# Moving rows of fp32 products in two halves of a tile, even columns in one and odd columns in the other

## The chip, the cores and the metric

The kernel runs on one core of a Trainium2 chip, as one program. The metric is device time in microseconds (us), the median of several runs. The core has engines with queues of their own: TensorE (PE) for matrix products, VectorE (DVE) and ScalarE (ACT) for elementwise work, SyncE (SP) whose queue issues nearly all transfers, and GpSimd (POOL), which is unused here. PE reads its operands from the on-chip memory SBUF, which has 128 partitions, and adds up results in banks of PSUM.

## What is computed

One layer of a streaming encoder on 1024 tokens of 1024 features, all in float32.

```python
h = h + 0.5 * swiglu_ffn(rmsnorm(h, norm_ffn1), ffn1_w_in, ffn1_w_out)
u = rmsnorm(h, norm_mix)
proj = u @ w_in
q, k, v, g_ret, p, gates = jnp.split(proj, split_points, axis=-1)
ret = retention(rotary(q), rotary(k) * RET_QK_DIM ** -0.5, v)
ret = ret * lax.rsqrt(jnp.mean(ret * ret, axis=-1, keepdims=True) + NORM_EPS)
ret = ret.reshape(b, s, RET_V) * jax.nn.silu(g_ret)
pool_out = multiscale_pool(p, pool_w, pool_scale)
gate = jax.nn.sigmoid(gates.reshape(b, s, N_BRANCH, D_MODEL) + gate_bias)
merged = gate[:, :, 0] * (ret @ w_ret_up) + gate[:, :, 1] * (pool_out @ w_pool_up)
h = h + merged @ w_out
h = h + 0.5 * swiglu_ffn(rmsnorm(h, norm_ffn2), ffn2_w_in, ffn2_w_out)
return rmsnorm(h, norm_final)
```

The feed-forward layers have 2816 hidden features, the retention 4 heads of 256.

## The kernel before

Features lie along the partitions and tokens along the columns: an activation is 8 tiles of 128 features by 1024 tokens. A product on PE has a stationary operand of 128 x 128 (the weights) and a moving operand of 128 x 512 (activations, 512 tokens of 128 features); its result adds to a PSUM bank of 128 x 512.

Float32 products are made of three products each. `split` (L160) writes a high part in the type float32r with a copy on ACT (L161), and the rest, source minus high part, with a subtraction on DVE (L162). `split_scaled` (L164) does the same with a factor per partition (L165 on ACT, L166 on DVE). `mm3` (L179) then adds three products: high by high (L181), high weights by low columns (L182), low weights by high columns (L183). PE loads 128 x 128 weights anew for each (PEld in the profile).

A moving operand is a tile of `mv` (L108), `[P, 2, H]`: 512 columns of the high part, 2048 bytes, and behind them the 512 columns of the low part. `parts(m)` gives the two, each read from its first column to its last. Weights lie in a tile of `wt` (L111) of four blocks of 128 columns for each part. A weight tile can be shifted in its place by `APART` = 22 columns, 88 bytes; this is done for the weights of `common` and for the operands of the retention that `pieces` cuts.

The stages, in order: feed-forward 1 (`ffn_in`, `ffn_out`), the projections (`values` and `pairs` of groups `project`), the retention with the pooling products put between (`retention`, `fillers`), merging and output projection (`two_by_two`), feed-forward 2. Large products go by Strassen's scheme with seven products in place of eight (`strassen`, steps `b1` to `b7`): `Next` makes the sums of activation blocks that they need, as moving operands, with `put` and `blocks`, and `prep_w` makes the sums of weights. Some of the seven are cut once more into products of 256 columns (`common`), whose moving operands are halves of such rows. `ffn_out` makes its moving operands with `operand` from spilled tiles. In `values` the roles are turned: the weights of the value projection are the moving operand, and the activations of 128 tokens at a time are loaded as weights, so results have tokens along the partitions; `store` spills them to DRAM, and `Unit.loads` reads them for the retention. In the retention itself q, k and v are made into rows with `operand` and read as weights and as moving operands.

The order of the work is set by the order of the code: `Flow.run` calls the preparing half of a step four steps ahead of its products (`LOOK` = 4) and takes deferred work from a queue, one or two items after each step. A tile scheduler lays the instructions on the engines by that order, with `high_priority` for what empties PSUM banks. Tiles come from rotating buffers: 28 of `mv`, 5 of `wt`, 4 of `raw`, 9 of `t4`, 8 of `c2`, and 8 PSUM banks.

Of the kernel before, what the change touches and what calls it, by code (L numbers as in the profile page):

```python
# [17 lines left out]
P = 128  # L18
# [72 lines left out]
def block_kernel(ctx: ExitStack, tc, x, x_tok, vecs, f1_in, f1_out, w_in, w_v, pool_w, w_ret, w_pool, w_o,  # L91
# [16 lines left out]
    def mv(name):  # L108
        return sb.tile([P, 2, H], F32R, tag="mv", bufs=N_MV, name=name)

    def wt(name, at=0):  # L111

        w = sb.tile([P, S + LINE], F32R, tag="wt", bufs=N_WT, name=name)
        return w[:, at : at + S].rearrange("p (z i c) -> p z i c", z=2, i=4)
# [35 lines left out]
        return t[:, j * H : (j + 1) * H]  # L150

    LO, HI = slice(0, HD), slice(HD, H)

    def half_of(t, j):
        return t[:, (LO, HI)[j]]
# [10 lines left out]
        stt(lo, src, by, hi.bitcast(F32), MUL, SUB)  # L166

    def operand(src, name):
        m = mv(name)
        split(m[:, 0], m[:, 1], src)  # L170
        return m
# [100 lines left out]
    class Next(Norm):  # L272
# [13 lines left out]
            self.square(mt, tokens, src)  # L286

        def put(self, n, i, src, by=None):
            m = mv(f"{self.name}{n}{i}")
            self.M[n, i] = m  # L290
            if by is None:
                split(m[:, 0], m[:, 1], src)
            else:
                split_scaled(m[:, 0], m[:, 1], src, by)

        def g(self, mt, v=None):
            if self.gain is None:
# [63 lines left out]
        def blocks(self, R, tags, over=False):  # L361

            left, x = dict(zip(("y3", "y2", "y4") if over else ("y1", "y3", "y2", "y4"), tags)), {}

            def sums(z):
                for i in range(2):
                    m = self.M[R, 2 * i + z]  # L370
                    v = c2(f"{self.name}x{i}{z}")
                    tt(v, m[:, 0].bitcast(F32), m[:, 1].bitcast(F32), ADD)
                    x.update({(i, j, z): half_of(v, j) for j in range(2)})

            def difference(n, z):

                x00, x01, x10, x11 = (x[i, j, z] for i in range(2) for j in range(2))
                to, p, q = {"y1": (x00, x01, x00), "y3": (x01, x11, x01), "y2": (x00, x11, x00),
                            "y4": (x00, x10, x00)}[n]
                tt(to, p, q, SUB)  # L380
                if n not in left:
                    m, at = self.M[R, z], HI
                else:
                    tag, bufs = left[n]
                    if (R, n) not in self.made:

                        self.made[R, n] = sb.tile([P, 2, H], F32R, tag=tag, bufs=bufs, name=f"{self.name}{R}{n}")
                    m, at = self.made[R, n], (LO, HI)[z]
                self.Y[R, n, z] = parts(m, at)
                split(m[:, 0, at], m[:, 1, at], to)  # L390
                if z and n == "y4":
                    self.ready.add(R)

            work = []
            for z in range(2):
                work.append(lambda z=z: (sums(z), difference("y1", z)))
                work.append(lambda z=z: difference("y3", z))
                work.append(lambda z=z: (difference("y2", z), difference("y4", z)))
            return work

        def block(self, R, n, z):

            if isinstance(n, str):
                flow.until(lambda: R in self.ready)
                return self.Y[R, n, z]
            return parts(self.operand(R, 2 * n[0] + z), (LO, HI)[n[1]])

        def work(self, *steps):

# [31 lines left out]
    def strassen(nx, wa, wb, name, evac, end, begin=None, shared=(), dest=None):  # L441
# [34 lines left out]

        def prod(dst, w, m, start, stop):
            for i in range(4):
                mm3(t[dst], parts(t["w", w], i), parts(nx.operand(m, i)), start and i == 0, stop and i == 3)

        def u(n):
            t[n] = c2(f"{name}{n}")
# [207 lines left out]
    def plain(M, nk, src, name, evac, begin, banks):  # L690

        t = {}
        for q in range(0, nk, 4):

            def prep(q=q):
                if q == 0:
                    t["raw"] = raw(f"{name}raw")
                    load(t["raw"][:, : nk * P], src)
                t[q] = weights(t["raw"][:, q * P : (q + 4) * P], f"{name}w{q}")
                if q + 4 == nk:  # L700
                    begin()

            def body(q=q):
                if q == 0:
                    t["dst"] = [f(f"{name}d{j}") for j, f in enumerate(banks)]
                for i in range(4):
                    w = parts(t[q], i)
                    m = [parts(M(q + i)[j]) for j in range(2)]
                    first, final = q + i == 0, q + i == nk - 1
                    for j in range(2):  # L710
                        mm(t["dst"][j], w[0], m[j][0], start=first, stop=False)
                        mm(t["dst"][j], w[0], m[j][1], start=False, stop=False)
                    for j in range(2):
                        mm(t["dst"][j], w[1], m[j][0], start=False, stop=final)
                if q + 4 == nk:
                    evac(t["dst"])

            yield prep, body
# [85 lines left out]
    def plain_group(nx, blocks, name, evac, end):  # L804

        t, w = {}, {}

        def step(o, i, j):


            def prep():
                if j == 0:
                    w[o, i] = weights(blocks[2 * o + i], f"{name}w{o}{i}")

            def body():
                if i == 0:
                    t[o] = bank(f"{name}{o}{j}")
                for k in range(4):
                    mm3(t[o], parts(w[o, i], k), parts(nx.operand(("R11", "R12", "R21", "R22")[2 * i + j], k)),
                        i == 0 and k == 0, i == 1 and k == 3)  # L820
                if i == 1:
                    evac((o, j), t[o], None)
                    if (o, j) == (1, 1):
                        end()

            return prep, body

        return [step(o, i, j) for j in range(2) for i in range(2) for o in range(2)]
# [4 lines left out]
    def ffn_out(nx, ops, ready, w, res, name, sink, end, last=None):  # L833
# [100 lines left out]
        def step(n, f, k, where, start, after):  # L934
            o = {}

            def prep():
                L, X = f(k)
                o["w"] = weights(L, f"{name}{n}w{k}")
                o["m"] = X if len(X.shape) == 3 else operand(X, f"{name}{n}m{k}")  # L940
                if n == "p3" and not last and k >= FH // 2:
                    z = k - FH // 2 + 1
                    ahead[z] = operand(t4s(z), f"{name}p4m{z}")

            def body():
                if start and k == 0:
                    for i in range(4):
                        bk[where, i] = (sum_bank if where == "b" and i < N_SUM else bank)(f"{name}{n}{where}{i}")
                for i in range(4):
                    mm3(bk[where, i], parts(o["w"], i), parts(o["m"]), start and k == 0, k == FH - 1)  # L950
                    if k == FH - 1:
                        after(i)

            return prep, body
# [81 lines left out]
        L, X = {}, {}  # L1036

        def turned(n, k):
            mm3(last.bank(n), parts(X[k], slice(n * P, (n + 1) * P)), parts(L[k]), False, k == FH - 1)

        def near(k):
            def prep():
# [204 lines left out]
    def values():  # L1247
# [36 lines left out]
        def step(L, R, k, where, start, after):  # L1284
            w = []

            def prep():
                t = weights(block(L, k), f"v{L}w{k}")
                w.extend(flat(t, z) for z in range(2))

            def body():
                if start and k == 0:
# [1 line left out]
                        bk[where, i] = (sum_bank if where == "b" and i < N_SUM else bank)(f"v{L}{i}")  # L1294
                m = nx.operand(R, k)
                for i in range(4):
                    mm3(bk[where, i], parts(m, slice(i * P, (i + 1) * P)), w, start and k == 0, k == 3)
                    if k == 3:
                        with soon():
                            after(i, bk[where, i])  # L1300
# [1 line left out]
            return prep, body  # L1302

        def store(o, j, i, src):
            to = vs[2 * o + j].rearrange("p (h t c) -> p h t c", h=2, t=4)
            load(to[:, :, i], src.rearrange("p (h c) -> p h c", h=2))
            if i == 3:
                stored.update(f"v{h}{j}" for h in (2 * o, 2 * o + 1))

# [71 lines left out]
    def pool(n):  # L1381
# [13 lines left out]
        def body():  # L1395
            for i in range(2):
                mt = 2 * n + i
                dst = [f(f"px{mt}{j}") for j, f in enumerate((sum_bank, bank))]
                for kt in range(2):
                    for j in range(2):  # L1400
                        mm3(dst[j], parts(w[0], 2 * kt + i), parts(Mg[kt][j]), kt == 0, kt == 1)
                M[mt] = []
                for j in range(2):
                    m = mv(f"po{mt}{j}")
                    with soon():
                        split_scaled(m[:, 0], m[:, 1], dst[j], vec[:, V_SCALE + mt : V_SCALE + mt + 1])
                    M[mt].append(m)

        return prep, body
# [67 lines left out]
    class Unit:  # L1477
# [42 lines left out]
            self.dec, self.ss, self.O, self.state, self.total, self.by = u.dec, u.ss, u.O, u.state, u.total, u.by  # L1520

        def values(self):
            self.V = [operand(half(self.src["v"], n), f"v{self.name}{n}") for n in range(2)]
            if self.nh == 0:
                self.by = sb.tile([P, 32], F32, tag="by", bufs=2, name=f"by{self.h}")
                for j in range(2):
# [10 lines left out]
            return col(self.by, z + 4 * (j % 2) + 2 * self.nh + j // 2)  # L1537

        def operands(self):
            self.Q = [operand(half(self.src["q"], i), f"q{self.name}{i}") for i in range(2)]  # L1540
            self.K = [operand(half(self.src["k"], i), f"k{self.name}{i}") for i in range(2)]

        def scores(self):

# [470 lines left out]
```

## Time and profile before

| | |
|---|---|
| median of 3 runs | 2138.09 us (2138.02 to 2139.77) |
| span of the profiled execution, first to last instruction | 2137.8 us |
| PE busy, products | 2127.8 us, 10798 instructions |
| PE busy, loading weights | 1808.3 us |
| DVE busy | 1873.2 us, 3352 instructions |
| ACT busy | 1100.9 us, 2082 instructions |
| mean granted PE clock | 0.999 |
| memory traffic | 313.60 MB, 147 GB/s on average |

The profile is one execution, as the hardware profiler saw it. Durations of products overlap, since they are pipelined: PE takes the next one while the last drains, so the time that a product costs is the distance from its start to the next start, not its duration. An idle time of an engine costs only what the chain to the end waits for.

### The profile page before, as it was taken

To read this page: it belongs to the slowest core of one execution; us is meant where nothing else is said; L and a number is where in the kernel's file an instruction comes from. 1 tells how busy PE (TensorE), PEld (TensorE's weight loads), DVE (VectorE), ACT (ScalarE), POOL (GpSimd) and SP (SyncE) were. 2 spreads that over 40 slices of the span, in tenths; PEclk is the share of its full clock that TensorE was granted. 3 is DMA by queue.
4 is the path that set the end of the run, shared out by engine and by line. 5 is a ranking of instruction groups with operands and counts; after the bars stand their busy time and mean duration, and the time that the engine had idled before them with its cause. 6 is when DMAs were issued, how large, how long until landed. Compare 5 with 4: busy or idle time off the path is not lost.

```text
span 2137.8 us, 30138 instructions
## 1 busy us (share of the span) xinstructions
PE 2127.8 (100%) x10798; PEld 1808.3 (85%) x10798; DVE 1873.2 (88%) x3352; ACT 1100.9 (51%) x2082; POOL 0.2 (0%) x4
## 2 busy tenths in 40 slices
PE   9999999999999999999999999999999999999998
PEld 7888888888888888888888998888888888888887
DVE  8798888997986799999988988899988988899796
ACT  8544444454654534454457753456644544455454
POOL 0000000000000000000000000000000000000000
PEclk9999999999999999999999999999999999999999
DMA  7232323675543333332336666624133232358542
GB/s 251 83 133 75 138 84 129 202 266 187 172 138 98 110 109 119 109 124 104 119 129 223 197 226 236 236 89 163 64 103 119 87 126 85 132 199 276 192 138 99
DMA packets 116391, 313.60 MB, mean 147 GB/s; under 512 B 12817, under 2 KB 17041, under 8 KB 116241
## 3 DMA queue, kind: packets, MB, share of 16 engines
q1 hardware_dynamic: 115664, 310.63, 42.7%
q8 instruction: 84, 1.38, 0.3%
q10 hardware_dynamic: 576, 1.05, 0.1%
q14 instruction: 67, 0.54, 0.1%
HBM read 220.93 MB, written 90.70 MB: 146 GB/s over the span
## 4 chain that ended last, share of the span: by engine, by line
PE 94%; DVE 4%; ACT 1%; DMA 1%; issue 0%; SPq 0%; ACTq 0%; DVEq 0%
PE c_b L181 2%; PE c_b L182 2%; PE c_b L183 2%; PE a_b L181 2%; PE a_b L182 2%; PE a_b L183 2%; PE c_e L182 2%; PE c_e L181 2%; PE c_e L183 2%; PE a_e L182 2%; PE a_e L181 2%; PE a_e L183 2%; PE a_a L181 1%; PE a_a L183 1%; PE a_a L182 1%; PE c_a L181 1%
## 5 line engine op out<-in xcount | busy, mean ns | idle before, releaser
L182 PE MATMUL c_b<-n3T,c_wS 128*128 128x512 f32 x176 | 68.6, 390 | 0.0
L183 PE MATMUL c_b<-n3T,c_wS 128*128 128x512 f32 x176 | 68.5, 389 | 0.0
L181 PE MATMUL c_b<-n3T,c_wS 128*128 128x512 f32 x176 | 68.4, 390 | 0.0
L182 PE MATMUL a_b<-n1T,a_wS 128*128 128x512 f32 x168 | 65.4, 389 | 0.0
L181 PE MATMUL a_b<-n1T,a_wS 128*128 128x512 f32 x168 | 65.4, 389 | 0.0
L183 PE MATMUL a_b<-n1T,a_wS 128*128 128x512 f32 x168 | 65.3, 389 | 0.0
L181 PE MATMUL a_a<-n1R,a_wL 128*128 128x512 f32 x120 | 46.7, 389 | 0.0
L182 PE MATMUL a_a<-n1R,a_wL 128*128 128x512 f32 x120 | 46.7, 389 | 0.0
L183 PE MATMUL a_a<-n1R,a_wL 128*128 128x512 f32 x120 | 46.7, 389 | 0.0
L182 PE MATMUL c_a<-n3R,c_wL 128*128 128x512 f32 x112 | 43.6, 389 | 0.0
L181 PE MATMUL c_a<-n3R,c_wL 128*128 128x512 f32 x112 | 43.6, 389 | 0.0
L183 PE MATMUL c_a<-n3R,c_wL 128*128 128x512 f32 x112 | 43.6, 389 | 0.0
L183 PEld LDWEIGHTS c_b<-n3T,c_wS 128*128 128x128 f32 x176 | 33.0, 188 | 6.9
L182 PEld LDWEIGHTS c_b<-n3T,c_wS 128*128 128x128 f32 x176 | 33.0, 188 | 6.8 <-DVE n3T L162 0.2
L181 PEld LDWEIGHTS c_b<-n3T,c_wS 128*128 128x128 f32 x176 | 33.0, 188 | 6.8 <-ACT n3T L161 0.3
L183 PEld LDWEIGHTS a_b<-n1T,a_wS 128*128 128x128 f32 x168 | 31.5, 188 | 6.6
L181 PEld LDWEIGHTS a_b<-n1T,a_wS 128*128 128x128 f32 x168 | 31.5, 188 | 6.5
L182 PEld LDWEIGHTS a_b<-n1T,a_wS 128*128 128x128 f32 x168 | 31.5, 188 | 6.3
L162 DVE TENSOR_TENSOR a_wS<-a_S,a_wS 128x512 fp32r<-128x512 f32 x45 | 31.0, 690 | 6.7 <-ACT a_wS L161 6.7
L161 ACT CAST c_wS<-c_S 128x512 fp32r<-128x512 f32 x46 | 27.9, 624 | 13.2 <-DVE c_S L455 7.1
L182 PE MATMUL c_e<-n3T,c_wL 128*128 128x512 f32 x88 | 34.5, 393 | 0.0
L181 PE MATMUL c_e<-n3T,c_wS 128*128 128x512 f32 x88 | 34.4, 391 | 0.0
(3385 smaller groups left out, 8156.9 us busy)
## 6 DMA issues: line engine op xcount, KB each, us to landing
c_ra<-in_f_in SPq DMA_DIRECT2D x22, 512.0 KB, 3.8
c_rb<-in_f_in SPq DMA_DIRECT2D x22, 512.0 KB, 3.7
a_ra<-in_f_in SPq DMA_DIRECT2D x21, 512.0 KB, 3.9
a_rb<-in_f_in SPq DMA_DIRECT2D x21, 512.0 KB, 3.9
t<-au SPq DMA_DIRECT2D x11, 512.0 KB, 2.8
b<-ag SPq DMA_DIRECT2D x11, 512.0 KB, 4.3
r<-au SPq DMA_DIRECT2D x11, 512.0 KB, 3.7
bra<-in_f_out SPq DMA_DIRECT2D x11, 512.0 KB, 6.3
```

The lines of the kernel that those rows point to most:

```text
L161: copy(hi, src)
L162: tt(lo, src, hi.bitcast(F32), SUB)
L181: mm(dst, w[0], m[0], start=start, stop=False, skip_group_check=True)
L182: mm(dst, w[0], m[1], start=False, stop=False, skip_group_check=True)
L183: mm(dst, w[1], m[0], start=False, stop=stop, skip_group_check=True)
```

## The change

Moving operands made by the new helper `rows` lie in a tile `[P, 2, 2, HD]`: the first index of two is the half of the tile (2048 bytes), the second the part, high or low, and 256 columns follow. `by_two` reads a source with a step of two columns, so that even columns go to the first half and odd ones to the second. `lay` gives one part in both halves, where the splits write. `moving` gives a part to PE in the order of the tokens: a column of the first half, the column at the same place in the second half, 2048 bytes on, and so forth.

```diff
+    def rows(name):
+        return sb.tile([P, 2, 2, HD], F32R, tag="mv", bufs=N_MV, name=name)
+    def lay(m, z, at=slice(None)):
+        return m[:, :, z, at]
+    def by_two(src):
+        return src.rearrange("p (a b) -> p b a", b=2)
+    def moving(m, at=slice(None)):
+        return [m[:, :, z, at].rearrange("p b a -> p a b") for z in range(2)]
...
     def operand(src, name):
+        m = rows(name)
+        split(lay(m, 0), lay(m, 1), by_two(src))
+        return m
+
+    def straight(src, name):
         m = mv(name)
         split(m[:, 0], m[:, 1], src)
         return m
...
         def put(self, n, i, src, by=None):
-            m = mv(f"{self.name}{n}{i}")
+            m = rows(f"{self.name}{n}{i}")
             self.M[n, i] = m
             if by is None:
-                split(m[:, 0], m[:, 1], src)
+                split(lay(m, 0), lay(m, 1), by_two(src))
             else:
-                split_scaled(m[:, 0], m[:, 1], src, by)
+                split_scaled(lay(m, 0), lay(m, 1), by_two(src), by)
...
-                mm3(t[dst], parts(t["w", w], i), parts(nx.operand(m, i)), start and i == 0, stop and i == 3)
+                mm3(t[dst], parts(t["w", w], i), moving(nx.operand(m, i)), start and i == 0, stop and i == 3)
```

The same replacement is made in `blocks`, `block`, `plain`, `plain_group`, `ffn_out`, `pool` and the last products (`turned`). The retention keeps the old layout through `straight`. In `values` the activations are loaded as weights, 128 contiguous columns of one half: 128 even tokens or 128 odd ones. So the rows of a result are every other token, and `store` writes each result with two transfers of 64 partitions that put the tokens back in their places:

```diff
-                    mm3(bk[where, i], parts(m, slice(i * P, (i + 1) * P)), w, start and k == 0, k == 3)
+                    mm3(bk[where, i], [m[:, i % 2, z, QUARTER[i // 2]] for z in range(2)], w, start and k == 0, k == 3)
...
-            to = vs[2 * o + j].rearrange("p (h t c) -> p h t c", h=2, t=4)
-            load(to[:, :, i], src.rearrange("p (h c) -> p h c", h=2))
+            to = vs[2 * o + j].rearrange("(a b) (h t c) -> b t a h c", b=2, h=2, t=4)
+            for z in range(2):
+                load(to[i % 2, i // 2 * 2 + z], src[z * P // 2 : (z + 1) * P // 2].rearrange("p (h c) -> p h c", h=2))
```

On PE the instructions and their order stay the same; 7812 products with 512 columns and 2184 with 256 read by turns. On DVE and ACT 358 splits change their shape. At the head of the program, where the first operands `n1R` are made from `x` and the weights `a_w` from `ra` and `rb`, DVE's queue stood so before:

```order
4 L162 TENSOR_TENSOR a_w_296<-ra,a_w_296 128x512
5 L166 SCALAR_TENSOR_TENSOR n1R_310<-x_92,vec,n1R_310 128x512
6 L166 SCALAR_TENSOR_TENSOR n1R_316<-x_93,vec,n1R_316 128x512
7 L166 SCALAR_TENSOR_TENSOR n1R_322<-x_94,vec,n1R_322 128x512
8 L166 SCALAR_TENSOR_TENSOR n1R_328<-x_95,vec,n1R_328 128x512
```

and with the change so:

```order
4 L179 TENSOR_TENSOR a_w_296<-ra,a_w_296 128x512
5 L183 SCALAR_TENSOR_TENSOR n1R_310<-x_92,vec,n1R_310 128x2x256
6 L183 SCALAR_TENSOR_TENSOR n1R_316<-x_93,vec,n1R_316 128x2x256
7 L183 SCALAR_TENSOR_TENSOR n1R_322<-x_94,vec,n1R_322 128x2x256
8 L183 SCALAR_TENSOR_TENSOR n1R_328<-x_95,vec,n1R_328 128x2x256
```

The place of each is the same; the moving operands are written as two blocks of 256, the weights as before.

SP's queue at the end of `values`, where `v_216` to `v_219` are the spilled values, `vc` their results, and `q0ra`, `q0rb`, `k0ra`, `k0rb` the weights of the next stage, stood so before:

```order
L140 DMA q0ra<-in_w_in 128x1024
L140 DMA v_217<-vc_6403 256x1x256
L140 DMA v_217<-vc_6408 256x1x256
L140 DMA v_217<-vc_6413 256x1x256
L140 DMA v_217<-vc_6418 256x1x256
L140 DMA q0rb<-in_w_in 128x1024
L140 DMA v_219<-vc_6428 256x1x256
L140 DMA v_219<-vc_6433 256x1x256
L140 DMA v_219<-vc_6438 256x1x256
L140 DMA v_219<-vc_6443 256x1x256
L140 DMA k0ra<-in_w_in 128x1024
L140 DMA k0rb<-in_w_in 128x1024
```

and with the change so:

```order
L156 DMA v_219<-vc_6430 64x2x256 x2
L156 DMA v_219<-vc_6435 64x2x256 x2
L156 DMA v_219<-vc_6440 64x2x256 x2
L156 DMA v_219<-vc_6445 64x2x256 x2
L156 DMA q0rb<-in_w_in 128x1024
L156 DMA v_216<-vc_6520 64x2x256 x2
L156 DMA v_216<-vc_6525 64x2x256 x2
L156 DMA v_216<-vc_6530 64x2x256 x2
L156 DMA k0ra<-in_w_in 128x1024
L156 DMA k0rb<-in_w_in 128x1024
```

Each store is two transfers now, the load of `q0rb` has moved behind the four results of `v_219`, and the loads of `k0ra` and `k0rb` behind three results of `v_216`.

More of the change, by code (lines that the diff above doesn't have):

```diff
@@ L152, in block_kernel @@
     LO, HI = slice(0, HD), slice(HD, H)
+    QUARTER = slice(0, P), slice(P, HD)
     def half_of(t, j):
@@ L370, in sums @@
                     m = self.M[R, 2 * i + z]
-                    v = c2(f"{self.name}x{i}{z}")
-                    tt(v, m[:, 0].bitcast(F32), m[:, 1].bitcast(F32), ADD)
-                    x.update({(i, j, z): half_of(v, j) for j in range(2)})
+                    v = c2(f"{self.name}x{i}{z}").rearrange("p (b a) -> p b a", b=2)
+                    tt(v, lay(m, 0).bitcast(F32), lay(m, 1).bitcast(F32), ADD)
+                    x.update({(i, j, z): v[:, :, QUARTER[j]] for j in range(2)})
             def difference(n, z):
@@ L381, in difference @@
                 if n not in left:
-                    m, at = self.M[R, z], HI
+                    m, at = self.M[R, z], QUARTER[1]
                 else:
@@ L385, in difference @@
                     if (R, n) not in self.made:
[L387 to L390, printed above, removed]
+                        self.made[R, n] = sb.tile([P, 2, 2, HD], F32R, tag=tag, bufs=bufs, name=f"{self.name}{R}{n}")
+                    m, at = self.made[R, n], QUARTER[z]
+                self.Y[R, n, z] = moving(m, at)
+                split(lay(m, 0, at), lay(m, 1, at), to)
                 if z and n == "y4":
@@ L405, in block @@
                 return self.Y[R, n, z]
-            return parts(self.operand(R, 2 * n[0] + z), (LO, HI)[n[1]])
+            return moving(self.operand(R, 2 * n[0] + z), QUARTER[n[1]])
         def work(self, *steps):
@@ L707, in body @@
                     w = parts(t[q], i)
-                    m = [parts(M(q + i)[j]) for j in range(2)]
+                    m = [moving(M(q + i)[j]) for j in range(2)]
                     first, final = q + i == 0, q + i == nk - 1
@@ L818, in body @@
                 for k in range(4):
-                    mm3(t[o], parts(w[o, i], k), parts(nx.operand(("R11", "R12", "R21", "R22")[2 * i + j], k)),
+                    mm3(t[o], parts(w[o, i], k), moving(nx.operand(("R11", "R12", "R21", "R22")[2 * i + j], k)),
                         i == 0 and k == 0, i == 1 and k == 3)
@@ L939, in prep @@
                 o["w"] = weights(L, f"{name}{n}w{k}")
-                o["m"] = X if len(X.shape) == 3 else operand(X, f"{name}{n}m{k}")
+                o["m"] = X if len(X.shape) == 4 else operand(X, f"{name}{n}m{k}")
                 if n == "p3" and not last and k >= FH // 2:
@@ L949, in body @@
                 for i in range(4):
-                    mm3(bk[where, i], parts(o["w"], i), parts(o["m"]), start and k == 0, k == FH - 1)
+                    mm3(bk[where, i], parts(o["w"], i), moving(o["m"]), start and k == 0, k == FH - 1)
                     if k == FH - 1:
@@ L1038, in turned @@
         def turned(n, k):
-            mm3(last.bank(n), parts(X[k], slice(n * P, (n + 1) * P)), parts(L[k]), False, k == FH - 1)
+            mm3(last.bank(n), parts(X[k], slice(n * P, (n + 1) * P)), moving(L[k]), False, k == FH - 1)
         def near(k):
@@ L1287, in prep @@
             def prep():
-                t = weights(block(L, k), f"v{L}w{k}")
-                w.extend(flat(t, z) for z in range(2))
+                t = sb.tile([P, S + LINE], F32R, tag="wt", bufs=N_WT, name=f"v{L}w{k}")
+                t = t[:, :S].rearrange("p (b z a) -> p b z a", b=2, z=2)
+                split(lay(t, 0), lay(t, 1), by_two(block(L, k)))
+                w.extend(moving(t))
             def body():
@@ L1400, in body @@
                     for j in range(2):
-                        mm3(dst[j], parts(w[0], 2 * kt + i), parts(Mg[kt][j]), kt == 0, kt == 1)
+                        mm3(dst[j], parts(w[0], 2 * kt + i), moving(Mg[kt][j]), kt == 0, kt == 1)
                 M[mt] = []
                 for j in range(2):
-                    m = mv(f"po{mt}{j}")
+                    m = rows(f"po{mt}{j}")
                     with soon():
-                        split_scaled(m[:, 0], m[:, 1], dst[j], vec[:, V_SCALE + mt : V_SCALE + mt + 1])
+                        split_scaled(lay(m, 0), lay(m, 1), by_two(dst[j]), vec[:, V_SCALE + mt : V_SCALE + mt + 1])
                     M[mt].append(m)
@@ L1522, in values @@
         def values(self):
-            self.V = [operand(half(self.src["v"], n), f"v{self.name}{n}") for n in range(2)]
+            self.V = [straight(half(self.src["v"], n), f"v{self.name}{n}") for n in range(2)]
             if self.nh == 0:
@@ L1539, in operands @@
         def operands(self):
-            self.Q = [operand(half(self.src["q"], i), f"q{self.name}{i}") for i in range(2)]
-            self.K = [operand(half(self.src["k"], i), f"k{self.name}{i}") for i in range(2)]
+            self.Q = [straight(half(self.src["q"], i), f"q{self.name}{i}") for i in range(2)]
+            self.K = [straight(half(self.src["k"], i), f"k{self.name}{i}") for i in range(2)]
         def scores(self):
```

## The prediction, made before the changed kernel had run

> **What bounds the kernel now.** I read the page first, then the waits of TensorE, then stretches of time.
>
> ```profile
> span 2137.8 us, 30138 instructions
> PE 2127.8 (100%) x10798; PEld 1808.3 (85%) x10798; DVE 1873.2 (88%) x3352; ACT 1100.9 (51%) x2082; POOL 0.2 (0%) x4
> PE 94%; DVE 4%; ACT 1%; DMA 1%; issue 0%; SPq 0%; ACTq 0%; DVEq 0%
> PE set L204 <- DVE zero L199: 1.2, 1, 1.2
> ```
>
> The third line is the chain that ended last, the fourth the longest wait of TensorE (PE) in the whole run: 1.2 us. PE carries 94% of the chain and has no waits worth removing. A busy PE is not a PE at its peak, though, so the question is how fast its products follow each other. Three stretches hold only products of 512 columns (columns of the rows: stretch, its length, PE busy with its count, PEld, DVE, ACT, POOL, granted clock, DMA share, GB/s):
>
> ```profile
> 550.00:600.00 50.00, 50.00 (x222) 41.42 (x221) 43.23 (x72) 30.07 (x55) 0.00 (x0) 1.00 0.60 196
> 650.00:700.00 50.00, 50.00 (x222) 41.41 (x221) 31.74 (x51) 18.33 (x33) 0.00 (x0) 1.00 0.34 108
> 1950.00:2000.00 50.00, 50.00 (x222) 41.39 (x221) 44.55 (x75) 26.50 (x47) 0.00 (x0) 1.00 0.72 238
> ```
>
> A product counts when any part of its 0.39 us lies in the stretch, so the pitch from start to start is 50.39 / 222 = 0.2270 us. It is the same with VectorE (DVE) busy for 31.7 or 44.6 us and DMA at 0.34 or 0.72: other traffic does not set it. Now two runs of products with 256 columns, and the first products of the program, which are bf16 with 512 columns (start, duration, engine, line, operation; a row "x2" gives the start of the first):
>
> ```profile
> 1650.36 0.28 PE L181 MATMUL c_x<-n3R21y,c_ws 128*128 128x256 f32 x1
> ...
> 1654.33 0.28 PE L183 MATMUL c_b<-n3R,c_ws 128*128 128x256 f32 x1
> 1231.95 0.28 PE L181 MATMUL ob<-state,q 128*128 128x256 f32 x1
> ...
> 1233.26 0.28 PE L183 MATMUL ob<-state,q 128*128 128x256 f32 x1
> 2.47 1.06 PE L204 MATMUL set<-zero 128*128 128x512 bf16 x2
> ...
> 4.60 0.97 PE L204 MATMUL set<-zero 128*128 128x512 bf16 x2
> 5.41 0.38 PE L204 MATMUL set<-zero 128*128 128x512 bf16 x1
> 5.63 0.38 PE L204 MATMUL set<-zero 128*128 128x512 bf16 x1
> ```
>
> The first run takes 3.97 us for 35 steps, 0.1134 us each, half of 0.2270: what is lost grows with the columns and is no fixed price of a product. The bf16 products start 0.426 us apart (2.13 us, five steps) and the last two 0.22 us apart, half as much, so PE doubled its rate there; half of 0.426 is 0.213 us for 512 columns. Against that, 0.2270 is 6.6% more: one lost slot in about 16 columns, that is in 64 bytes of fp32. The second run, whose weights begin on a 64-byte multiple instead of 24 bytes past one, takes 1.31 / 11 = 0.119 us: where PE's reads lie in memory shows in the pitch. So PE is held by reading four-byte moving columns, not by its array and not by another engine.
>
> **The change, part by part.** *Products.* In the changed program 7812 products of 512 columns and 2184 of 256 read two places 2048 bytes apart by turns; 528 of the retention, the transposes and sums stay. Number and order stay. No row shows PE reading by turns, so its price has to be bounded. Below: nothing is lost, 0.213 us. Above: each column costs two slots, as in the rows 0.426 us apart. The case for a gain: each 64-byte piece now lasts 32 slots instead of 16, so the next one has twice the time to come, and the bf16 products, which also take 32 columns from 64 bytes, show 0.22. I take 0.216, between 0.213 and that row, and half of it, 0.108, for 256 columns:
> - 7812 x (0.2270 - 0.216) = 86 us
> - 2184 x (0.1134 - 0.108) = 12 us
>
> That is 98 us of PE, 95.2% of its time in such stretches.
>
> *What is late next.* DVE. These are the stretches where it is fullest:
>
> ```profile
> 750.00:950.00 200.00, 199.94 (x1004) 169.64 (x1003) 194.65 (x336) 93.50 (x186) 0.00 (x0) 1.00 0.31 111
> 1400.00:1550.00 150.00, 149.40 (x663) 122.44 (x662) 146.96 (x251) 93.00 (x169) 0.00 (x0) 1.00 0.31 109
> 100.00:150.00 50.00, 50.00 (x240) 41.55 (x238) 48.33 (x91) 23.61 (x44) 0.00 (x0) 1.00 0.44 158
> 400.00:450.00 50.00, 50.00 (x242) 42.16 (x242) 48.46 (x83) 24.17 (x45) 0.00 (x0) 1.00 0.80 278
> 1900.00:1950.00 50.00, 50.00 (x243) 42.20 (x242) 49.05 (x83) 24.93 (x46) 0.00 (x0) 1.00 0.79 277
> 2050.00:2100.00 50.00, 50.00 (x232) 41.55 (x231) 48.23 (x83) 31.83 (x60) 0.00 (x0) 1.00 0.47 153
> ```
>
> At 95.2%, PE would need 190.3, 142.7 and four times 47.6 us. DVE's work stands over that by 4.3, 4.2, 0.7, 0.9, 1.4 and 0.6 us: 12 us given back, less if work slides into the emptier stretches beside them, more if DVE cannot be filled to the brim.
>
> *Splits.* 358 pairs of a ScalarE (ACT) and a DVE instruction that make a moving operand now read the source with a step of 8 bytes and write two blocks; the number of instructions does not change.
>
> ```profile
> L162 DVE TENSOR_TENSOR a_wS<-a_S,a_wS 128x512 fp32r<-128x512 f32 x45 | 31.0, 690 | 6.7 <-ACT a_wS L161 6.7
> L755 DVE TENSOR_TENSOR cg<-cg,n3rb 128x1024 f32<-128x1024 f32 x17 | 20.8, 1223 | 0.0
> L161 ACT CAST a_wS<-a_S 128x512 fp32r<-128x512 f32 x45 | 27.3, 623 | 13.2 <-PE a_a L183 6.8 <-DVE a_S L455 3.4 <-PE a_e L183 2.1
> L763 ACT ACTIVATE cg<-cg 128x1024 f32<-128x1024 f32 x22 | 23.4, 1063 | 8.2 <-DVE cg L755 7.1 <-DVE cg L758 1.0
> ```
>
> No row reads with a step either. 512 further elements cost DVE 0.533 us and ACT 0.440 us, so the bounds for all 358 are nothing, and one slot lost per element: 191 us of DVE, 158 us of ACT. ACT, at 51%, hides its part; DVE would not. I take nothing, since the elements are as many as in the rows at 690 and 623 ns; the upper end is a rival below.
>
> *Stores of the values.* 16 transfers become 32 of half the rows, and SP's queue issues the weights of `q0` and `k0` later.
>
> ```profile
> L140 SPq DMA_DIRECT2D v<-vc x16: 512/551/822, 683.6 to 711.3; - x16
> 691.16 0.33 SPq L140 DMA_DIRECT2D k0ra<-in_w_in  x1
> 697.21 14.59 SPq L140 DMA_DIRECT2D v<-vc  x8
> 713.20 0.39 PE L181 MATMUL k0a<-n2R,k0wL 128*128 128x512 f32 x1
> ```
>
> Sixteen more issues of about 0.55 us are 8.8 us of a queue that waits for the results anyway. The load of `k0ra`, issued at 691.2 now, comes behind three stores of the last groups: first start 697.2, six issues, 700.5. PE first needs what is made of it at 713.2, so some 12 us hide the transfer and two splits. I take nothing; without that cover PE would lose up to those 9 us once.
>
> Sum: 98 - 12 = 86 us off the span of 2137.8, and 0.3 us lie between this execution's span and the median of the runs, 2138.09. **Forecast: 2052 us.**
>
> **The rivals.** *Alternating costs a slot per column (slower).* Every column then goes to another place than the one before it. If what now costs a slot every 16 columns is the change of place, the pitch becomes 0.426 and 0.213: 7812 x 0.199 + 2184 x 0.0996 = 1772 us more, 3910 us. It decides from the point where a turn costs more than a sixteenth of a slot. For it: the pitch reacts to addresses (0.119 against 0.1134). Against it: the loss has a grain of 64 bytes and not of single columns, and in the run at 0.119 us a second stream, the weights, is read from elsewhere between the columns, and that loses 0.0056 us, one more slot in about 19 columns, not one in every column. [...]
>
> *Nothing changes on PE.* If the lost slot comes after so many columns or bytes, wherever they lie, the pitch stays at 0.227, the rest is hidden, and the time is 2138 us. For it: 256 and 512 columns lose in proportion, at any load. Against it: the bf16 pair at 0.22, with as many columns.
>
> *The splits cost their upper bound.* DVE then has 1873 + 191 = 2064 us of work; at the share it reaches between 750 and 950 us, 194.65 / 200, that takes 2121 us, whatever PE gains. For it: DVE is the next engine. Against it: only a lost slot on every element gives it.
>
> **How the numbers follow.** Chances: forecast 0.66, splits 0.06, no change 0.10, alternating slower 0.18. I lean to the forecast because the loss sits in the reading and has a grain that the change stretches to twice the time, and keep nearly a fifth for the rival because no row shows such a read. The likeliest case by itself runs from 2014 us (pitch 0.213: 109 + 15 us, all work of DVE hidden) to 2093 us (half of the 98 us, with 4 us given back). The range that takes in the splits and no change is 2014 to 2142; only the slow rival lies outside. A difference under 0.2%, some 4 us, is about what a measurement of this kernel cannot tell from none. Faster by more: 0.66 + 0.06 = 0.72; within: 0.10; slower: 0.18.
>
> **What would show it.** In stretches of 512-column products, the count in 50 us: 222 now, some 233 at 0.216, 119 at 0.426. In the runs of 256 columns, 0.108 against 0.1134. The rows of the splits should stay at 690 and 623 ns. DVE should stand near 50 of 50 us in the six stretches above, with new waits of PE on DVE there. The retention's products should keep their pitch. A pitch below 0.227 with a span that hardly moves would say that DVE, not PE, binds; a changed pitch of the weight loads alone would say that I put the loss on the wrong stream.

## The result and the profile after

| | before | after |
|---|---|---|
| median | 2138.32 us (2138.02 to 2139.77, 4 runs) | 2113.83 us (2112.26 to 2115.5, 4 runs) |
| ratio, with its 95% interval | | 0.9884 (0.987 to 0.9898) |
| span of the profiled execution | 2137.8 us | 2111.2 us |

The change gains 24.5 us, 1.2%. The prediction was 2052 us, 86 us of gain. The busy times of the changed kernel, from its page:

```profile
span 2111.2 us, 30162 instructions
PE 2058.6 (98%) x10798; PEld 1817.2 (86%) x10798; DVE 1909.9 (90%) x3352; ACT 1167.1 (55%) x2082; POOL 0.2 (0%) x4
```

PE is busy 69 us less than before. DVE is busy 37 us more and ACT 66 us more, with the same number of instructions. First the pitch of PE: a stretch that it fills with products of 512 columns (columns as in the prediction: stretch, length, PE, PEld, DVE, ACT, POOL, granted clock, DMA share, GB/s), and the first and the last row of a run of 256-column products (start, duration, engine, line, operation):

```profile
500.00:550.00 50.00, 50.00 (x234) 43.82 (x233) 42.28 (x65) 25.68 (x39) 0.00 (x0) 1.00 0.52 162
...
1624.85 0.27 PE L203 MATMUL c_x<-n3R,c_wx 128*128 128x256 f32 x1
...
1628.09 0.28 PE L205 MATMUL c_a<-n3R,c_ws 128*128 128x256 f32 x1
```

50.38 / 234 = 0.215 us, against 0.2270 before; over the whole trace 0.2158, where 0.216 was predicted. The run of 256 columns takes 3.24 us for 29 steps, 0.1117 each: less than the 0.1134 of before, but not the 0.108 of the prediction. So PE does read faster by turns. Then four stretches that the prediction showed, and one more, which stood so before:

```profile
600.00:650.00 50.00, 50.00 (x221) 41.05 (x221) 47.50 (x79) 28.16 (x50) 0.00 (x0) 1.00 0.34 117
```

With the change:

```profile
550.00:600.00 50.00, 47.71 (x214) 41.21 (x213) 44.76 (x69) 34.11 (x53) 0.00 (x0) 0.97 0.59 195
650.00:700.00 50.00, 47.99 (x223) 41.67 (x222) 25.03 (x38) 20.67 (x30) 0.00 (x0) 0.97 0.47 127
750.00:950.00 200.00, 196.03 (x1035) 172.83 (x1034) 195.71 (x342) 95.74 (x192) 0.00 (x0) 1.00 0.36 124
1400.00:1550.00 150.00, 139.79 (x624) 116.92 (x623) 142.38 (x236) 92.11 (x155) 0.00 (x0) 0.98 0.32 109
600.00:650.00 50.00, 45.53 (x206) 38.12 (x205) 49.84 (x75) 33.49 (x46) 0.00 (x0) 1.00 0.20 68
```

Between 550 and 600 us, where PE was full before with 222 products, it now idles and does 214. From 1400 to 1550 us it idles 10 us. From 600 to 650 DVE fills 49.84 of 50 us with 75 instructions, where 79 took 47.50 before. The longest wait of PE was 1.2 us before. Now some are longer (who waits, for whom; total, times, longest):

```profile
PE c_a L203 <- ACT c_b L514: 3.5, 1, 3.5
PE c_x L203 <- ACT cg L601: 3.2, 6, 0.6
PE vL L204 <- DVE vL11w L179: 2.6, 1, 2.6
...
PE bp5a L203 <- DVE bd L986: 2.3, 1, 2.3
```

The first names ACT. What stands behind it shows in time order, on PE, then DVE, then ACT (start, duration, engine, line, operation, idle time before it and its releaser):

```profile
1488.76 0.38 PE L205 MATMUL c_a<-n3R,c_wL 128*128 128x512 f32 x1
1492.65 0.79 PE L203 MATMUL c_a<-n3R,c_wL 128*128 128x512 f32 x1 [3.51 <-ACT c_b L514]
1493.24 0.63 PE L204 MATMUL c_a<-n3R,c_wL 128*128 128x512 f32 x1
1493.67 0.63 PE L205 MATMUL c_a<-n3R,c_wL 128*128 128x512 f32 x1
...
1488.07 0.90 DVE L179 TENSOR_TENSOR n3T<-wo,n3T 128x512 fp32r<-128x512 f32 x1
1488.82 0.75 DVE L477 TENSOR_TENSOR c_S<-c_rb 128x512 f32<-128x512 f32 x1
1489.42 0.75 DVE L1821 TENSOR_TENSOR wo<-wo3b,wo 128x512 f32<-128x512 f32 x1
1490.02 0.75 DVE L477 TENSOR_TENSOR c_S<-c_S,c_ra 128x512 f32<-128x512 f32 x1
...
1490.85 0.62 ACT L178 CAST c_wS<-c_S 128x512 fp32r<-128x512 f32 x1 [3.87 <-DVE c_S L477]
1491.46 0.66 ACT L178 CAST n3T<-wo 128x512 fp32r<-128x512 f32 x1
1492.02 0.58 ACT L514 COPY c_b<-c_a 128x512 f32<-128x512 f32 x1
```

DVE has no gap. The copy that PE needs stands in ACT's queue behind the cast of `c_wS`, which has idled 3.87 us for a sum of weights, `c_S`, that DVE reached at 1490.02. ACT, busy 55%, only passes DVE's delay on. And behind the wait PE's products start 0.59 and 0.43 us apart; 0.43 is half of its rate. The granted clock, the share of its full clock that PE is given, is 0.93 on average from 1450 to 1500 us; the trace has it at one half from 1491.7 to 1498.5 us.

With the starts of all products, PE's time can be divided into three: the pitch that each shape has when nothing disturbs it (small deviations included), the gaps, and the extra time of products at half rate. A pitch over 1.35 times the usual one counts as a gap, which takes in single products that start some 0.1 us late (after 44 products of 512 columns in the change, the next starts 0.32 to 0.34 us later at the full clock); it counts as half rate where the trace has the granted clock at one half. The rest of a span, 29 to 33 us, is its head, its tail and a few other shapes. In us, for this pair and for the experiments below:

| profiled execution | span | at the usual pitch | gaps | half rate |
|---|---|---|---|---|
| before | 2137.8 | 2094.9 | 13.9 | 0 |
| after | 2111.2 | 2001.1 | 73.4 | 7.5 |
| E1, no step, PE by turns | 2074.5 | 2000.9 | 44.0 | 0 |
| E2, step, PE straight | 2137.4 | 2093.9 | 14.6 | 0 |
| E4, turned at PSUM, PE by turns | 2074.0 | 2000.9 | 43.8 | 0 |
| E5, written by turns, PE by turns | 2183.2 | 2001.3 | 124.1 | 24.9 |
| E7, E4 with less work on DVE | 2055.8 | 2000.4 | 26.2 | 0 |
| E8, written by turns, PE straight | 2222.6 | 2094.9 | 79.3 | 17.8 |

The products gained 93.8 us; gaps took 59.5 of it and the half rate 7.5, so 26.8 us are left. The spans differ by 26.6.

Why DVE and ACT are later shows in the splits. One group, `n2T`, before and after (count, then min/median/max in ns, first and last start):

```profile
L161 ACT CAST n2T<-bacc x12: 613/621/623, 614.0 to 659.5; 128x512 fp32r<-128x512 f32 x12
...
L162 DVE TENSOR_TENSOR n2T<-bacc,n2T x12: 686/692/708, 614.7 to 660.5; 128x512 fp32r<-128x512 f32 x12
```

```profile
L178 ACT CAST n2T<-bacc x12: 662/881/917, 599.4 to 649.7; 128x512 fp32r<-128x512 f32 x12
...
L179 DVE TENSOR_TENSOR n2T<-bacc,n2T x12: 712/830/884, 600.5 to 650.8; 128x512 fp32r<-128x512 f32 x12
```

The same elements cost ACT 42% more and DVE 20% more. Over all the splits of moving operands that read SBUF, 302 on each engine without a factor, the medians went from 618 to 876 ns on ACT and from 689 to 830 on DVE. The splits that read PSUM with the same step (16, `po`) did not move: 746 ns on DVE before and after.

### The profile page after: what moved, and what is told of

It is laid out like the page before. It is cut to its first block, busy times and chain, and to the rows that moved or that the text cites. A ratio compares the mean times of both kernels' runs of the same rounds, so it can differ in the third digit from the quotient of the medians.

```text
span 2111.2 us, 30162 instructions
## 1 busy us (share of the span) xinstructions
PE 2058.6 (98%) x10798; PEld 1817.2 (86%) x10798; DVE 1909.9 (90%) x3352; ACT 1167.1 (55%) x2082; POOL 0.2 (0%) x4
## 5 line engine op out<-in xcount | busy, mean ns | idle before, releaser
L204 PE MATMUL c_b<-n3T,c_wS 128*128 128x512 f32 x176 | 67.0, 381 | 0.0
L205 PE MATMUL c_b<-n3T,c_wS 128*128 128x512 f32 x176 | 66.8, 379 | 0.0
L203 PE MATMUL c_b<-n3T,c_wS 128*128 128x512 f32 x176 | 66.6, 380 | 0.2 <-ACT n3T L178 0.2
L203 PE MATMUL a_b<-n1T,a_wS 128*128 128x512 f32 x168 | 63.7, 379 | 0.0
L204 PE MATMUL a_b<-n1T,a_wS 128*128 128x512 f32 x168 | 63.7, 379 | 0.0
L205 PE MATMUL a_b<-n1T,a_wS 128*128 128x512 f32 x168 | 63.7, 379 | 0.0
L179 DVE TENSOR_TENSOR c_wS<-c_S,c_wS 128x512 fp32r<-128x512 f32 x46 | 32.1, 700 | 3.0 <-ACT c_wS L178 2.9
```

Source lines behind the costliest of these rows:

```text
L179: tt(lo, src, hi.bitcast(F32), SUB)
L203: mm(dst, w[0], m[0], start=start, stop=False, skip_group_check=True)
L204: mm(dst, w[0], m[1], start=False, stop=False, skip_group_check=True)
L205: mm(dst, w[1], m[0], start=False, stop=stop, skip_group_check=True)
```

## The experiments

Three things in the change could slow the splits: the step of 8 bytes in their source, the two blocks that they write, and PE's own reading by turns beside them. The first four kernels separate these.

**E1: no step in the source.** The splits write the two halves of a tile from the two halves of the source. PE reads by turns as before; the columns of the outputs stand in another order.

```diff
     def by_two(src):
-        return src.rearrange("p (a b) -> p b a", b=2)
+        return src.rearrange("p (b a) -> p b a", b=2)
```

> The changed kernel with one edit: the splits send columns 0 to 255 to the first half and 256 to 511 to the second, so that no source is read with a step; products still read the halves by turns, so that the columns of the results come in another order than the reference's and the output differs. Theory A (most of the expected gain is lost because splits of SBUF sources with a step of 8 bytes take 141 ns more on VectorE and 254 ns more on ScalarE, and operands come late): splits return to about 690 and 622 ns, VectorE's busy time from 1910 to about 1870 us, PE's long waits shrink to a third, the time falls to 2045 to 2080 us. Rival B (VectorE and ScalarE are too full for a faster PE, whatever a split costs): the splits get shorter, but the time stays at 2095 to 2114 us.

Measured: 2077.52 us (2076.29 to 2078.98, 4 runs), ratio 0.9715 (0.97 to 0.9729). The splits' medians are 617 ns on ACT and 681 on DVE, no longer than the 618 and 689 before the change. Theory A holds: PE's longest wait behind the head is 1.7 us instead of 3.5, and gaps and half rate fall from 80.9 to 44.0 us. So neither the two blocks that are written nor PE's turns slow a split that reads in a row, and without the step the change is worth 61 us.

**E2: the step alone.** The splits are those of the change, but PE reads the first half and then the second.

```diff
-        return [m[:, :, z, at].rearrange("p b a -> p a b") for z in range(2)]
+        return [m[:, :, z, at] for z in range(2)]
```

> The changed kernel with products that read the first half and then the second, each from its first column to its last; the splits keep their step. The order of the columns of the results differs from the reference's. It shows the price of the splits alone at the old pitch. Theory A: the pitch of 512 columns is back at 0.227 us; the longer splits are mostly hidden behind it, but not at the changes of stage, where operands are made in bursts: 2145 to 2175 us, slower than before. Rival B (the splits cost nothing by themselves): 2136 to 2142 us, as before. Rival C (the pitch hangs on the layout of the tile and not on reading by turns): the pitch stays at 0.216.

Measured: 2139.21 us (2138.51 to 2140.43, 10 runs), ratio 1.0003 (0.9993 to 1.0012). PE's pitch is 0.227 us again. The group `n2T`, from the durations of the two lines:

```profile
L178 ACT CAST n2T<-bacc x12: 656/664/669, 613.2 to 658.8; 128x512 fp32r<-128x512 f32 x12
...
L179 DVE TENSOR_TENSOR n2T<-bacc,n2T x12: 677/682/692, 613.9 to 659.9; 128x512 fp32r<-128x512 f32 x12
```

By itself the step costs ACT 46 ns in the median of the 302 splits, DVE nothing, and no time. That the splits are slow by themselves is refuted: the large price comes only while PE reads by turns. E1, E2 and the two kernels of the study make a square:

| medians: time; split on ACT, on DVE | PE reads straight | PE reads by turns |
|---|---|---|
| source in a row | 2138.9 us; 618, 689 ns | 2077.5 us; 617, 681 ns |
| source with the step | 2139.2 us; 664, 683 ns | 2113.8 us; 876, 830 ns |

Alone, turns give 61 us and the step costs no time; together 36 us are lost. The changed kernel shows the same inside one run. Splits of the 302 during which PE started fewer than one product a microsecond took 658 ns on ACT (8 of them) and 685 on DVE (15) in the median; where PE started more than four, they took 878 and 833. The cast of `n3T` at 1491.46 us above, 0.66 us long while PE waits, is one of the first kind.

**E3: another distance.** The halves lie 1024 bytes apart instead of 2048.

```diff
-        return m[:, :, z, at]
+        return m[:, z, :, at]
...
-        return [m[:, :, z, at].rearrange("p b a -> p a b") for z in range(2)]
+        return [m[:, z, :, at].rearrange("p b a -> p a b") for z in range(2)]
```

> The changed kernel with the two halves of one part beside each other: products read by turns two places 1024 bytes apart, not 2048. If reading by turns is all that counts, the pitch of 512 columns stays at 0.216 us and the time at 2105 to 2120 us. If the distance of 2048 bytes matters (two places that do not disturb each other), the pitch is higher: 0.227 us or more, and the time 2140 us or far above.

Measured, in a single run: 2112.78 us, pitch 0.216 and 0.112 us, `n2T` 879 ns on ACT and 817 on DVE. Of these two distances of the halves, neither changes the gain or the loss.

**E4: the turn made where PSUM is emptied.** Activations lie in SBUF with the even tokens first. Whatever empties a bank reads it with a step of two columns; the splits read in a row. Every result is computed as in the change. Some 45 lines are changed, most of them like these:

```diff
-        split(lay(m, 0), lay(m, 1), by_two(src))
+        split(lay(m, 0), lay(m, 1), tok(src))
...
-                copy(u("p7"), t["e"])
+                copy(tok(u("p7")), cols(t["e"]))
```

Here `tok` cuts a row into its two halves, and `cols` takes the even columns of a bank, then the odd ones.

> A version that computes the reference with products by turns and without a step in SBUF: the halves hold columns 0 to 255 and 256 to 511, the results lie in PSUM in the order of the turns, and whatever empties a PSUM bank reads it with a step of two columns and writes the tokens back in order; the stores of the values are as before the change. In the changed kernel the 16 splits whose source is in PSUM took 745 and 693 ns with a step, 746 and 691 without. Theory A: reading PSUM with a step stays free, so the time is that of the run without a step, 2045 to 2080 us. Rival B: 2095 to 2114 us. If reading PSUM with a step costs something after all, evacuations get longer than 689 ns on VectorE and 587 ns on ScalarE and PE waits for banks.

Measured: 2077.35 us (2074.79 to 2081.33, 4 runs), ratio 0.9718 (0.9702 to 0.9734), faster than both kernels of the study. A copy on ACT that reads a bank with the step, and a split of this kernel on DVE:

```profile
L544 ACT COPY c_p<-c_e x22: 569/588/590, 1482.2 to 1842.8; 128x512 f32<-128x512 f32 x22
...
L187 DVE TENSOR_TENSOR n2T<-bacc,n2T x12: 674/676/680, 591.7 to 637.4; 128x512 fp32r<-128x512 f32 x12
```

The copy's median is 588 ns, against 587 for the same copy without the step before. The addition `cu` of such a bank on DVE has 690 ns against 692. So on ACT and on DVE a step on the PSUM side costs nothing here.

**E5: the step moved to the writing side.** ACT and DVE read the source in a row, and write one column to the first half, the next to the second.

```diff
+    def turns(m, z):
+        return m[:, :, z].rearrange("p b a -> p a b")
     def by_two(src):
-        return src.rearrange("p (a b) -> p b a", b=2)
+        return src.rearrange("p (a b) -> p a b", b=2)
...
-        split(lay(m, 0), lay(m, 1), by_two(src))
+        split(turns(m, 0), turns(m, 1), by_two(src))
```

> The changed kernel with the step moved from the reading to the writing side of the splits: ACT and DVE read a source column after column, and write (DVE: also read the high part) in the order of the tokens, one column in the first half, the next 2048 bytes on. PE reads by turns as in the change; every result is computed as there. Theory (only stepped READS of a source, 8 bytes on, collide with PE's turns, writes do not): splits on ACT back near 617 ns, DVE between 681 and 830 because it reads the high part by turns, time 2077 to 2095. Rival (any access of ACT or DVE that leaves a run of bytes after each column collides with PE's turns): ACT at 850 ns or more, DVE at 830 or more, time 2114 or above.

Measured: 2184.13 us (2182.03 to 2184.94, 4 runs), ratio 1.021 (1.0195 to 1.0226): slower than before the change. `n2T` again:

```profile
L182 ACT CAST n2T<-bacc x12: 1112/1156/1207, 616.2 to 675.3; 128x512 fp32r<-128x512 f32 x12
...
L183 DVE TENSOR_TENSOR n2T<-bacc,n2T x12: 1100/1168/1292, 617.3 to 676.6; 128x512 fp32r<-128x512 f32 x12
```

My theory, that only stepped reads suffer, fell. The rival's time and durations hold; whether its reason, PE's turns, holds as well is for E8.

**E8: its control.** The splits of E5, with PE reading straight as in E2; the columns of the results stand in another order.

```diff
-        return [m[:, :, z, at].rearrange("p b a -> p a b") for z in range(2)]
+        return [m[:, :, z, at] for z in range(2)]
```

> The control to the kernel that writes by turns: ACT and DVE write (and DVE reads the high part) by turns as there, but PE reads the first half and then the second, so the columns of the results stand in another order. Theory (ACT and DVE are slowed only where PE reads by turns): splits near 617 to 665 ns on ACT and 681 to 750 on DVE, pitch of PE 0.227 us, time 2139 to 2143. Rival (jumps of 2048 bytes from element to element cost ACT and DVE by themselves): ACT at 1100 ns or more, DVE near 1135 as with PE by turns, time 2145 or above.

Measured: 2228.71 us (2225.03 to 2230.16, 4 runs), ratio 1.0422 (1.0405 to 1.044).

```profile
L182 ACT CAST n2T<-bacc x12: 1142/1160/1250, 629.8 to 689.8; 128x512 fp32r<-128x512 f32 x12
...
L183 DVE TENSOR_TENSOR n2T<-bacc,n2T x12: 1130/1246/1474, 631.0 to 691.0; 128x512 fp32r<-128x512 f32 x12
```

The splits are as slow without PE's turns as with them: 1164 and 1153 ns in the median of the 302, against 1143 and 1135 in E5. The theory of this run fell, its rival holds. So there are two costs, not one. Jumps of 2048 bytes from element to element cost ACT and DVE by themselves: 526 and 454 ns more for 512 elements in E5 than in E1, where 512 further elements cost 440 and 533 ns in the prediction's rows. (DVE also reads the high part so.) A step of 8 bytes is dear only beside PE's turns: 876 and 830 ns, against 664 and 683 in E2. Between E8 and E5 the turns of PE still bring 45 us.

**E6: the place of the weights.** E4 with the weights of the 256-column products on a 64-byte multiple.

```diff
-LINE, APART = 64, 22
+LINE, APART = 64, 0
```

> Kernel e4 (sources in order, PE by turns, time 2077) with the weights of the 256-column products on a 64-byte multiple instead of 24 bytes past one (also those of the retention). In the kernel before, such a place of the weights cost 0.119 against 0.1134 us for 256 columns in a row. Theory A (what collides there is weights with moving columns that lie in a row; by turns there is nothing left to collide): pitch of 256 columns by turns stays at 0.112, time within 3 us of e4 plus what the retention loses (264 products x 0.006 = under 2 us). Theory B (the shift also matters by turns): pitch 0.115 to 0.120, some 2184 x 0.004 to 0.008 = 9 to 17 us slower, 2086 to 2094. Theory C (the shift is what costs by turns: 0.112 instead of 0.108): pitch 0.108 to 0.110, 4 to 9 us faster.

Measured: 2079.83 us (2078.53 to 2081.12, 2 runs), ratio 0.9724 (0.9705 to 0.9744); the pitch by turns stays at 0.112 us, the retention's 256 columns in a row go from 0.118 to 0.120 in the median, since the groups whose operands lose the shift, such as `ob<-v,sm`, go from 0.115 to 0.120. Theory A holds: by turns the place of the weights does not matter, and it is not what keeps the pitch above 0.108.

**E7: less work for DVE.** E4 with the low part of each tile of weights made by a copy on ACT; the subtraction is left out.

```diff
     def weights(src, name, at=0):
...
-        split(flat(w, 0, n), flat(w, 1, n), src)
+        copy(flat(w, 0, n), src)
+        copy(flat(w, 1, n), src)
```

> Kernel e4 (2077 us) with the low part of every tile of weights made by a copy on ACT instead of a subtraction on DVE: that leaves out the subtraction, so the low parts are not remainders and the outputs differ; numbers of products and bytes stay. It takes some 230 instructions of 0.68 us, 150 us, off DVE and puts 140 us on ACT, which has room (1094 of 2074 us). In e4 waits of PE and products at half rate after them come to 44 us, against 14 in the kernel before. Theory (DVE, full in places, is what PE waits for): they fall to 10 to 20 us, time 2045 to 2058. Rival (PE waits for chains of instructions one after the other, not for the amount of DVE's work; a chain through ACT is as long): time 2070 or more.

Measured: 2056.92 us (2055.61 to 2057.62, 4 runs), ratio 0.9615 (0.9599 to 0.9631). The edit moved more than expected, 796 instructions; from its page:

```profile
span 2055.8 us, 29992 instructions
PE 2035.6 (99%) x10798; PEld 1814.9 (88%) x10798; DVE 1429.1 (70%) x2556; ACT 1467.5 (71%) x2878; POOL 0.2 (0%) x4
```

DVE lost 437 us and ACT took 373, and the gaps fell from 43.8 to 26.2 us (none of the 43.8 is at half rate, although the expectation counts such products in). The time fell by 20 us, inside the 2045 to 2058 of the theory, the gaps by less than it said. So about 20 us of E4 go with DVE's work on the weights. Whether its amount costs them, or that a low part is handed from ACT to DVE, this run does not separate. The rest is not settled either: with DVE at 70%, PE still waits 12 us more than before the change, for instance 1.7 us each for the copies of `ru0b` and `wo2b` on ACT. A chain of instructions one after the other has less cover when PE is faster, but ACT's own extra work in E7 could do the same.

## Why the prediction was wrong

- **Products: right in size, the reason open.** 0.2158 us where 0.216 was predicted; all products gained 93.8 us where the sum had 98. Its second term, 256 columns, was too large: 0.1117 instead of 0.108. Over all 2184 products the mean pitch, without gaps, went from 0.1144 to 0.1116 us, some 6 us instead of 12. By turns, half of the columns take more than half of the pitch: 0.1117 x 2 is 0.2234, against 0.2158. E2 and E3 show that the order of reading brings the gain. That it does so because each 64-byte piece lasts twice as long, as the prediction argued, no run tested.
- **Splits: the step that failed.** The prediction took "nothing, since the elements are as many as in the rows at 690 and 623 ns". They are as many, and by themselves they cost almost as much (E2). But beside PE's turns a split cost DVE 141 ns and ACT 258 ns more than before in the median. Summed over 302 of the pairs that is some 40 us and 77 us, and through waits of PE 36 us of time (after against E4 or E1). The two changes were priced each by itself, against rows in which neither took place; the price lies between them. The bounds that the prediction set, 191 and 158 us, held.
- **What is late next: right in kind, too small.** DVE was to give back 12 us. Even without the step (E4), the gaps are 43.8 us against 13.9: 30 us. The sum compared DVE's work with PE's in six stretches. It left out that PE waits in stretches where DVE is not full on average, here one of E4. It also left out that PE can run at half rate after a wait. That has no part in these 30, for E4's granted clock is 1.00 in every 50 us up to 2050 us; in the change itself it costs 7.5 us, which the 37 below take in.

```profile
600.00:650.00 50.00, 47.84 (x219) 40.84 (x219) 44.57 (x73) 28.27 (x51) 0.00 (x0) 1.00 0.21 70
```

- Together: 98 less 12 less 0 were predicted, 86 us; 94 less 30 less 37 were measured, 27 us in the profiled executions.
- **Stores of the values: right.** `k0ra` was issued late, but its first pair of splits ended at 698.4 us, and PE took the result up at 702.69 without a wait.

```profile
L178 ACT CAST k0wL<-k0ra x2: 617/628/640, 696.2 to 701.8; 128x512 fp32r<-128x512 f32 x2
L179 DVE TENSOR_TENSOR k0wL<-k0ra,k0wL x2: 687/688/689, 697.7 to 702.8; 128x512 fp32r<-128x512 f32 x2
...
702.69 0.38 PE L203 MATMUL k0a<-n2R,k0wL 128*128 128x512 f32 x1
```

- **The rivals.** "Alternating costs a slot per column" did not happen to PE; E5 and E8 show it on ACT and DVE, where writing by turns takes 1143 and 1135 ns in the median instead of 617 and 681. "Nothing changes on PE" fell. "The splits cost their upper bound" was the rival nearest to what happened, at a fraction of its price, and for another reason than a lost slot on every element.
- The range, 2014 to 2142 us, held the time. The likeliest case's own range ended at 2093 and missed it, since it gave the splits no price at all although no row showed a read with a step.

## What to carry to other kernels

When one change gives two engines new access patterns on the same memory, price the pair and not each alone: measure a kernel with each pattern by itself and one with both, and look at the durations of instructions that were not meant to change. Put a reordering where it costs nothing: here in the reading of PSUM (588 ns for a copy on ACT, against 587), not in the reading or writing of SBUF (splits of 876 and 1143 ns on ACT, against 617, while PE reads by turns). And when the busiest engine gets faster, count every queue that hands on a delay of the next one, and look for stretches at half of the clock behind new waits (17 us and 38 products in the change). A slow start of one product is not yet such a stretch: the granted clock tells.

## What the runs showed of the hardware

- **PE reads four-byte columns faster by turns from two places than in a row**: 0.2158 us against 0.2270 for 512 columns, at 1024 as at 2048 bytes between the places. 0.1117 against 0.1134 for 256. E2, with the same tiles and PE reading straight, is back at 0.227, so it is the order of reading. ACT's and DVE's writes by turns lose instead: 617 to 1143 ns and 681 to 1135 (E5 against E1).
- **PE's reading can slow ACT and DVE**: with an 8-byte step, 664 to 876 ns on ACT and 683 to 830 on DVE when only PE's pattern, and with it its pitch, changes (E2 against after). The faster pitch alone does not do it: in E1, at 0.2158 us, splits that read in a row stay at 617 and 681 ns. GpSimd is idle here, 0.2 us in the whole span. By what way PE's reading slows the other two was not tried.
- **After a wait of some microseconds PE can start again at half rate**, 0.427 us per 512 columns. In the change the granted clock is one half in four stretches, 17 us together, about the ends of waits of 3.51, 2.29, 2.01 and 1.98 us; 38 products in them cost 7.5 us more. It does not follow every such wait: one of 2.60 us in the change and one of 2.59 in E7 have none, one of 1.67 in E6 has. What decides is not shown. A new wait can cost more than its own length.
